# RWKV in units of 256 tokens on one chain, and the 24 matmuls of a weight panel's group kept together, in a two-layer decoder on one Trainium2 core

## The chip, the cores and the metric

The kernel runs on one core of a Trainium2 chip. A core has five engines with queues of their own: TensorE (matmuls, PE in the rows, with its weight loads shown apart as PEld), VectorE (DVE), ScalarE (ACT), GpSimd (POOL) and SyncE (SP, which issues the DMA transfers here). Each takes its instructions in the order that was fixed when the program was built, and waits on semaphores of the others. The metric is the device time of one execution in microseconds; before the change it is 3608.89 us, the median of three runs (3601.26 to 3626.65).

## The reference, cut to what matters

Two decoder layers run over 2048 prompt tokens and over 8 sample sequences of 8 tokens, with the same weights. Each layer projects its normalized input once, runs four recurrent mixers side by side (retention, HGRN2, GLA, RWKV-7), gates and joins their outputs, projects them back, and attends to 256 memory tokens.

```python
def mixer(h, l, pos, st, v_first, P):
    proj = h @ P['w_in'][l]
    p_ret, p_hgrn, p_gla, p_rwkv = jnp.split(proj, [...], axis=-1)
    ...
    o, s_hgrn = chunked_gated_linear(...)
    ...
    o_rwkv, s_rwkv, new_shift, v_first = rwkv_branch(p_rwkv, ...)
    out = jnp.concatenate([o_ret, o_hgrn, o_gla, o_rwkv], axis=-1) @ P['w_out'][l]

def rwkv7_scan(r, w, k, v, kk, a, s0):
    def step(S, inp):
        rt, wt, kt, vt, kkt, at = inp
        sa = jnp.einsum('bhvk,bhk->bhv', S, kkt)
        S = (S * wt[:, :, None, :] - sa[..., None] * (kkt * at)[:, :, None, :]
             + vt[..., None] * kt[:, :, None, :])
        return S, jnp.einsum('bhvk,bhk->bhv', S, rt)
    ...
```

## The kernel before, in words

The prompt is cut into four blocks of 512 tokens, and each layer goes through the four blocks in turn, so there are eight block steps. A block step (`block`, `gates`, `finish`) has this work:

- **Panel matmuls.** The input projection, the gates and the output projection multiply by weight panels. Each fp32 weight is split into two parts (tile `whl`, high and low) and so is the activation (`act`), and three of the four products are kept. One output group is 8 pieces of the contraction times 3 products, so 24 matmuls in a row into one PSUM tile `psd` (`group`, called by `dense_c` with 512 columns and by `dense_t` with 256). PSUM has two such tiles.
- **RWKV** (`R_rwkv`, with `invert` for the inverse of a triangular matrix by doubling). It works on units of 128 tokens: a unit holds two chunks of 64 and four heads, so the tile `NA` has four blocks on each half of the partitions. Inside `invert` the steps alternate between TensorE (`Xb,XB` and `Wb,XB` products, transpositions of `X`) and copies on VectorE and ScalarE (`Xb`, `Wb`, `XB`, a masked copy into `X`). The state `H` goes from chunk to chunk. The four units of a block are written one after the other, but odd and even units have tiles of their own (class `Turn` adds 0 or 1 to each tag) and PSUM tiles of their own (lane `a` for even units, `c` for odd ones), so two units can be under way at once.
- **GLA, HGRN, retention.** Each works on halves of 256 tokens. GLA and HGRN use `dyadic`: per level, two sets of small products (`dn_hq,dn_hf` for HGRN, 16 matmuls of 64x64 by 32 columns) go into PSUM lane `b`, masked copies put them into `sT`, and a key step and a query step on VectorE scale the operands for the next level. Then come outputs, state updates (`S_hgrn`, `S_ret`) and a head norm (`osb`, `hst`, `hss`, `rsq`, `hri`).
- **Output projection** (`w_out`), cross-attention to the memory, and the norm of the next block's input (`pre_norm`, interleaved through `ahead`).

What sets the order on an engine is a scheduler that runs when the program is built. It takes, of the instructions whose operands are there by its own clock, the one that stands first by priority; priority is the place in the code plus the offsets of the table `PRI`. `held` changes this for matmuls and transpositions: it counts matmuls that are recorded one after the other, and lifts each of them by `HOLD` except every `run[0]`-th one. A lifted matmul comes before everything else, so a run of `run[0]` matmuls can't be broken by others, and at the run's end another instruction may come in between. `run[0]` is `DENSE`, 12, for all matmuls, and `group` begins a new count.

Of the kernel before, what the change touches and what calls it, by code (L numbers as in the profile page):

```python
# [10 lines left out]
F32 = mybir.dt.float32  # L11
# [32 lines left out]
DENSE = 12  # L44
# [12 lines left out]
def shape_constants(seq, past):  # L57
    f = np.float32
    c = {}
# [67 lines left out]
    c["reset"] = np.broadcast_to((np.arange(128) % 64 != 0).astype(f), (128, 128)).copy()  # L127
    c["resets"] = np.broadcast_to((np.arange(SN) % SL != 0).astype(f), (128, SN)).copy()
    return c


class Turn:


    def __init__(self, pool, i):
        self.pool, self.i = pool, i

    def tile(self, shape, dtype, name, tag, bufs=None):
        return self.pool.tile(shape, dtype, name=name, tag=f"{tag}{self.i}", **({"bufs": bufs} if bufs else {}))
# [3 lines left out]
def decoder(ctx, tc, I, C, O):  # L143
# [73 lines left out]

    run = [DENSE, 0, None]

# [685 lines left out]
    def invert(NA, smp, wp):  # L905
# [4 lines left out]
        nb = P // 32  # L910
        blk = [slice(32 * b, 32 * b + 32) for b in range(4)]
        pair = wp.tile([128, 2, 4, 32], F32, name="X", tag="wt1")[:P]
        X, XT = pair[:, 0], pair[:, 1]
        pair = wp.tile([128, 4, 64], F32, name="XB", tag="kk")
        ND = pair[:P, 0:2].rearrange("p a (b n) -> p (a b) n", b=2)
        XB = pair.rearrange("p a n -> p (a n)")[:, 128:128 + P].rearrange("p (b n) -> p b n", b=nb)
        out = wp.tile([128, 4, 64], F32, name="XT", tag="wt2")
        flat = lambda x: x.rearrange("p q n -> p (q n)")

# [4 lines left out]
        tt(V, XT, ND, bc(K["x1"][:P].unsqueeze(1), [P, 4, 32]), ALU.mult)  # L924
        tt(V, XT, XT, bc(K["I32"][:P].unsqueeze(1), [P, 4, 32]), ALU.add)
        V.transpose(flat(X), flat(XT))
        Xb = wp.tile([128, 4, nb, 32], F32, name="Xb", tag="EA")[:P]
        Wb = wp.tile([128, nb, 4, 32], F32, name="Wb", tag="WU")
# [3 lines left out]
        def diagonal(dst, x, n):  # L932

            for b in range(n):
                o, i = dst[blk[b], :, b, :], x[blk[b]]
                if b % 2:
                    V.tensor_copy(o, i)  # L937
                else:
                    A.activation(o, i, AF.Copy)  # L939

        def turned():
            pt = PS("r")[:, :P]
            tr(pt, flat(X), P)
            diagonal(Xb, X, nb)
            A.activation(flat(XB), pt, AF.Copy)
        for li in range(1, 3 if smp else 5):
            turned()
            pw = PS("r")[:, :P].rearrange("p (b n) -> p b n", b=nb)
            for q in range(4):
                mm(flat(pw)[blk[q]], ND[:, q, :], flat(Xb[:, q]))  # L950
            diagonal(Wb, pw, 4)
            pz = PS("r")[:P, :128].rearrange("p (q n) -> p q n", q=4)
            for b in range(nb):
                mm(flat(pz)[blk[b]], XB[:, b, :], flat(Wb[:, b]))
            V.copy_predicated(X, bc(lmask[:P, li].unsqueeze(1), [P, 4, 32]), pz)  # L955
# [6 lines left out]
        low = wp.tile([128, 2, 64], F32, name="XL", tag="rx")  # L962
        G.tensor_copy(low[:, :, 32:64], bc(K["I32"].unsqueeze(1), [128, 2, 32]))
        pw = PS("r")[:, :64].rearrange("p (e n) -> p e n", e=2)
        for q in range(4):
            mm(pw[blk[q]], NA[:, q, 0, 32:64], Xb[:, q, 0:4:2, :])
        for q in range(4):
            V.tensor_copy(Wb[blk[q], 1:4:2, q, :], XB[blk[q], 1:4:2, :])
        A.activation(low[:, :, 0:32], pw, AF.Copy)
        pz = PS("r")[:, :128].rearrange("p (q n) -> p q n", q=4)  # L970
        for e in range(2):
# [1050 lines left out]
```

## Time and profile before

| what | value |
|---|---|
| median of three runs | 3608.89 us |
| the profiled execution, its own time | 3606.38 us |
| its span | 3604.6 us |
| TensorE busy | 3396.8 us (94%) |
| VectorE busy | 2280.4 us (63%) |
| ScalarE busy | 1392.1 us (39%) |
| GpSimd busy | 561.4 us (16%) |
| mean granted TensorE clock | 0.976 of full speed |
| HBM traffic | 146 GB/s over the span |

Busy time is the union of an engine's instructions. Matmuls are pipelined, and the time from the start of one to its end is longer than the distance between two starts, so a busy TensorE can hold more or fewer matmuls. The granted clock has two levels, 2.4 GHz (1.0) and 1.2 GHz (0.5). In the rows, `L230 MATMUL psd<-act,whl 128*128 128x512` is a matmul at line 230 that writes tile `psd` from `act` and `whl`, uses 128 rows by 128 columns of the array, and has 512 columns of moving data. A small fp32 matmul shows as two in the trace (`x8` for four in the code).

### The profile page before, as it was taken

The page shows a single profiled execution, that of the slowest core. Times are in us where ns is not written, and L with a number is a line of the kernel's source. Part 1 is how long each engine was busy: PE and PEld are TensorE (multiplying, and loading weights), DVE is VectorE, ACT ScalarE, POOL GpSimd, SP SyncE. Part 2 cuts the span into 40 slices and gives each one's busy share as a digit, 9 for nine tenths or more (in the row PEclk, how much of TensorE's full clock was granted, in tenths as well). Part 3 has the DMA queues.
Part 4 walks back from the last instruction along what each step waited for, and adds up shares of the span by engine and source line. Part 5 has one row for each costly group of instructions (what it writes and reads, how often), then busy time and mean ns, then how long its engine had stood idle before and what let it go on. Part 6 is the DMA issues. An engine that isn't in the chain of part 4 may idle for free.

```text
span 3604.6 us, 88705 instructions
## 1 busy us (share of the span) xinstructions
PE 3396.8 (94%) x36362; PEld 2817.2 (78%) x36362; DVE 2280.4 (63%) x7543; ACT 1392.1 (39%) x3489; POOL 561.4 (16%) x760
## 2 busy tenths in 40 slices
PE   7999999999999999999999999999889999999998
PEld 5767787777877888788877778778777778877887
DVE  4677645876337754786457865468744677547754
ACT  4452334522244324532445433453214442354323
POOL 3323331020000100110122233101200011000100
PEclk9998999999999999999999999999989999999999
DMA  6432675236652254324542348531554522542254
GB/s 190 151 107 81 187 242 193 72 100 202 212 200 72 100 192 148 113 87 171 180 159 83 103 137 267 172 132 66 160 189 167 170 86 94 193 172 86 73 199 184
DMA packets 244156, 530.92 MB, mean 147 GB/s; under 512 B 66983, under 2 KB 181927, under 8 KB 199719
## 3 DMA queue, kind: packets, MB, share of 16 engines
q1 hardware_dynamic: 243750, 525.25, 42.8%
q8 instruction: 287, 4.70, 0.5%
q14 instruction: 119, 0.97, 0.1%
HBM read 410.04 MB, written 115.16 MB: 146 GB/s over the span
## 4 chain that ended last, share of the span: by engine, by line
PE 73%; DVE 14%; ACT 5%; issue 4%; DMA 2%; POOL 1%; SPq 0%; ACTq 0%; POOLq 0%; DVEq 0%
PE psd L230 40%; PE psc L230 12%; PE psa L230 10%; PE psb L230 5%; PE psc L272 2%; PE psa L272 2%; PE psb L272 2%; DVE rsq L236 1%; DVE Wb L937 1%; DMA wraw<-in_w_in 1%; ACT Xb L939 1%; DVE hri L292 1%; DVE sT L745 1%; DVE hss L561 1%; DVE osb L236 0%
## 5 line engine op out<-in xcount | busy, mean ns | idle before, releaser
L230 PE MATMUL psd<-act,whl 128*128 128x512 f32 (+1 forms) x4032 | 1020.3, 405 | 22.7 <-DVE th L1266 9.6
L230 PEld LDWEIGHTS psd<-act,whl 128*128 128x128 f32 (+1 forms) x4032 | 751.6, 191 | 199.4 <-issue 17.4
L230 PE MATMUL psd<-whl,act 128*128 128x256 f32 x3840 | 544.7, 293 | 5.2 <-POOL whl L236 3.4
L230 PEld LDWEIGHTS psd<-whl,act 128*128 128x128 f32 x3840 | 485.9, 194 | 27.4 <-issue 9.8
L236 POOL TENSOR_TENSOR whl<-wraw,whl 128x1024 fp32r<-128x1024 f32 (+1 forms) x90 | 218.2, 2429 | 335.3 <-ACT whl L358 303.6
L230 PE MATMUL psd<-whl,oh 128*128 128x256 f32 x1152 | 211.6, 284 | 1.2 <-DMA whl<-w_w_out 1.2
L280 POOL TENSOR_TENSOR ri<-ri,mhalf 128x1 f32<-128x1 f32 (+1 forms) x87 | 49.2, 566 | 1039.4 <-DVE ri L279 1005.5
L230 PEld LDWEIGHTS psd<-whl,oh 128*128 128x128 f32 x1152 | 177.5, 189 | 2.6 <-DMA whl<-w_w_out 0.9
L230 PE MATMUL psd<-whl,ol 128*128 128x256 f32 x576 | 162.8, 283 | 0.0
L939 ACT ACTIVATE Xb<-X 32x128 f32<-32x128 f32 x324 | 99.1, 306 | 126.0 <-DVE X L955 78.1
L358 ACT ACTIVATE whl<-wraw 128x1024 fp32r<-128x1024 f32 (+1 forms) x90 | 94.1, 1049 | 124.4 <-PE psa L230 42.4
L745 DVE COPY_PREDICATED sT<-upack,psb 128x128 f32<-128x128 uint8 x320 | 92.6, 326 | 33.1 <-PE psb L230 29.5
L236 DVE TENSOR_TENSOR x<-x,psd 128x256 f32<-128x256 f32 x72 | 30.3, 421 | 128.3 <-PE psd L230 128.3
L230 PEld LDWEIGHTS psd<-whl,ol 128*128 128x128 f32 x576 | 108.6, 189 | 0.4 <-DVE ol L236 0.4
L230 PE MATMUL psb<-dn_hq,dn_hf 64*64 64x32 f32 (+1 forms) x3840 | 99.9, 225 | 7.8 <-DVE dn_hq L236 5.0
L230 PEld LDWEIGHTS psb<-dn_hq,dn_hf 64*64 64x64 f32 x3840 | 82.4, 137 | 31.0 <-issue 17.9
L435 ACT ACTIVATE xs<-xn 128x1024 f32<-128x1024 f32 (+1 forms) x34 | 35.8, 1054 | 155.4 <-PE psb L272 151.2
L1266 DVE SCALAR_TENSOR_TENSOR th<-th,psd 128x512 f32<-128x512 f32 x48 | 32.4, 686 | 91.8 <-ACT th L1265 91.8
L230 PE MATMUL psd<-hts,wraw 128*64 128x64 f32 x1984 | 84.1, 229 | 3.4 <-DVE th L1266 3.4
L230 PEld LDWEIGHTS psd<-hts,wraw 128*64 128x64 f32 x1984 | 69.9, 139 | 21.4 <-issue 11.0
L230 PE MATMUL psa<-whl,oh 128*128 128x256 f32 x448 | 82.8, 283 | 0.0
L230 PE MATMUL psc<-whl,oh 128*128 128x256 f32 x448 | 82.7, 283 | 0.0
(760 smaller groups left out, 7302.3 us busy)
## 6 DMA issues: line engine op xcount, KB each, us to landing
whl<-w_w_out SPq DMA_DIRECT2D x56, 1024.0 KB
wraw<-in_w_in SPq DMA_DIRECT2D x76, 512.0 KB
wraw<-in_w_out SPq DMA_DIRECT2D x32, 512.0 KB
w_w_out<-whl SPq DMA_DIRECT2D x16, 1024.0 KB
x<-x SPq DMA_DIRECT2D x32, 512.0 KB
whl<-w_rw_r SPq DMA_DIRECT2D x12, 1024.0 KB
whl<-w_rw_k SPq DMA_DIRECT2D x12, 1024.0 KB
whl<-w_rw_v SPq DMA_DIRECT2D x12, 1024.0 KB
```

The source lines that it names most:

```text
L230: PE.matmul(out, lhsT=lhsT, rhs=rhs, start=start, stop=stop, skip_group_check=True)
L236: e.tensor_tensor(out, a, b, op)
L272: PE.transpose(out, in_, ident[:rows, :rows])
L280: G.tensor_tensor(y, y, mhalf[:P], ALU.pow)
L292: V.scalar_tensor_tensor(y, t, 1.5, y, ALU.add, ALU.mult)
L358: A.activation(hl[:, 0], raw, AF.Copy)
L435: A.activation(out, xt, AF.Square, accum_out=ss[:P])
L561: V.tensor_reduce(ss[:P, :n4], sq[:P, :n4], AX.X, ALU.add)
L745: V.copy_predicated(out, bc(mk, [P, w, 32 // s, s]), ps)
L937: V.tensor_copy(o, i)
L939: A.activation(o, i, AF.Copy)
L1266: V.scalar_tensor_tensor(th, th, 1.0, x, ALU.add, ALU.mult)
```

## The change

RWKV's unit becomes 256 tokens (`nu = 2`, so four chunks and, in `invert`, eight blocks `m` in two groups `ng`), so a block has two units, and they share one set of tiles and both lanes: one unit runs after the other. Operations on VectorE and ScalarE are twice as wide and half as many; products that have their own 32 or 64 columns stay as many. `DENSE` becomes 24, and it holds only inside `group` and for each token tile in `w_out`; all other matmuls get runs of `SMALL`, 48. The core of the diff:

```diff
-DENSE = 12
+DENSE = 24
+SMALL = 48
...
-class Turn:
...
-    run = [DENSE, 0, None]
+    run = [SMALL, 0, None]
...
     def group(out, pairs):
         n = len(pairs)
-        run[2] = None
+        run[:] = DENSE, 0, None
         for i, (a, b) in enumerate(pairs):
             mm(out, a, b, i == 0, i == n - 1)
-        run[2] = None
+        run[:] = SMALL, 0, None
...
+        m = NA.shape[1]
+        ng = m // 4
...
         def turned():
-            pt = PS("r")[:, :P]
-            tr(pt, flat(X), P)
-            diagonal(Xb, X, nb)
-            A.activation(flat(XB), pt, AF.Copy)
+            pt = PS("r")[:, :ng * P]
+            for g in range(ng):
+                tr(pt[:, g * P:(g + 1) * P], flat(four(X, g)), P)
+            diagonal(lambda b: Xb[blk[b], :, b, :], lambda b: X[blk[b]], nb)
+            A.activation(XB.rearrange("p g b n -> p (g b n)"), pt, AF.Copy)
         for li in range(1, 3 if smp else 5):
             turned()
-            pw = PS("r")[:, :P].rearrange("p (b n) -> p b n", b=nb)
-            for q in range(4):
-                mm(flat(pw)[blk[q]], ND[:, q, :], flat(Xb[:, q]))
-            diagonal(Wb, pw, 4)
...
+            pw = PS("r")[:, :ng * P].rearrange("p (g b n) -> p g b n", g=ng, b=nb)
+            for g in range(ng):
+                for q in range(4):
+                    mm(flat(pw[:, g])[blk[q]], ND[:, 4 * g + q, :], flat(Xb[:, 4 * g + q]))
+            diagonal(lambda q: Wb[blk[q], :, :, q, :], lambda q: pw[blk[q]], 4)
...
-        nu = 1
-        P = n = 64 * ne
+        nu = 1 if smp else 2
+        P = 64 * ne
+        n = nu * P
...
-            for u in range(NT):
-                wp = Turn(wk, u % 2)
+            for u in range(NT // 2):
                 vfb = None
                 if l > 0:
-                    vfb = wp.tile([128, 2, 128], F32, name="vfb", tag="vT")
-                    dma(vfb, vf[b][:, :, u * 128:(u + 1) * 128])
-                with on_lane("ac"[u % 2]):
-                    R_rwkv(l, pr, st["H"], rk, on["rwkv"], wp, u, vfb)
+                    vfb = wk.tile([128, 2, 256], F32, name="vfb", tag="vT")
+                    dma(vfb, vf[b][:, :, u * 256:(u + 1) * 256])
+                R_rwkv(l, pr, st["H"], rk, on["rwkv"], wk, u, vfb)
...
                     for t in ts:
+                        run[:] = DENSE, 0, None
                         for n, k in enumerate(ks):
```

The order of TensorE in the third token block of layer 0, inside RWKV's `invert`, where its levels stand between GLA products (`qx`, `dn_qk`) and panels (`whl`). First before:

```order
L230 MATMUL psc<-Wb,XB 32x128 x4
L230 MATMUL psb<-qx_15036,dn_qk 64x64 x8
L230 MATMUL psa<-Wb,XL 64x128 x2
L230 MATMUL psa<-vT,LK 64x64 x8
L272 MATMUL psa<-fpack,ar 128x128 x2
L272 MATMUL psc<-fpack,X 128x128
L230 MATMUL psc<-Xb,XB 32x128 x4
L230 MATMUL psd<-whl,act 128x256 x12
L230 MATMUL psa<-Z,XT 64x128 x8
L230 MATMUL psc<-Wb,XB 32x128 x4
```

The same engine and block after the change:

```order
L221 MATMUL psa<-Xb,XB 32x128 x8
L221 MATMUL psd<-whl,act 128x256 x24
L221 MATMUL psc<-Wb,XB 32x128 x8
L221 MATMUL psb<-qx_13483,dn_qk 64x64 x8
L221 MATMUL psd<-whl,act 128x256 x24
L263 MATMUL psa<-fpack,X 128x128 x2
L221 MATMUL psc<-Xb,XB 32x128 x8
```

Where two units in lanes `a` and `c` stood between each other with half a panel group, there is now one unit with twice the matmuls in a step, and a whole group behind nearly every step.

The second place, on TensorE in the same block, is the second half of HGRN (`dn_hq,dn_hf`, the products of its levels) with retention (`S_ret`, `dn_rv`, `rqT`). First before:

```order
L230 MATMUL psb<-dn_hq,dn_hf 64x32 x16
L230 MATMUL psd<-act,whl 128x512 x12
L230 MATMUL psb<-dn_hq,dn_hf 64x32 x16
L230 MATMUL psd<-act,whl 128x512 x12
L230 MATMUL psb<-dn_hq,dn_hf 64x32 x16
L230 MATMUL psd<-act,whl 128x512 x12
L230 MATMUL psb<-dn_hq,dn_hf 64x32 x16
L230 MATMUL psd<-act,whl 128x512 x12
L230 MATMUL psb<-dn_hq,dn_hf 64x64 x8
```

The same engine and place after the change:

```order
L221 MATMUL psb<-dn_hq,dn_hf 64x32 x16
L221 MATMUL psc<-S_ret,rqT 64x128 x2
L221 MATMUL psc<-dn_rv,sT 64x64 x4
L221 MATMUL psb<-dn_hq,dn_hf 64x32 x16
L221 MATMUL psc<-S_ret,rqT 64x128 x2
L221 MATMUL psc<-dn_rv,sT 64x64 x4
L263 MATMUL psc<-fpack,dn_rq 128x128 x4
L221 MATMUL psb<-dn_hq,dn_hf 64x32 x80
L263 MATMUL psa<-fpack,osb 128x128 x4
L263 MATMUL psa<-fpack,dn_rk 128x128 x4
L221 MATMUL psb<-dn_hq,dn_hf 64x64 x8
```

The panel groups that stood between the levels now stand earlier, between steps of RWKV and GLA, and the levels follow each other with only small matmuls between them (`x80` is five levels in a row).

## Rows read from the trace of the kernel before

**Rows 1.** The page: the span, and each engine's busy time, share and instructions.
```profile
span 3604.6 us, 88705 instructions
PE 3396.8 (94%) x36362; PEld 2817.2 (78%) x36362; DVE 2280.4 (63%) x7543; ACT 1392.1 (39%) x3489; POOL 561.4 (16%) x760
```

**Rows 2.** Busy time by stretch: third block; VectorE's busiest 120 us; 2603 to 2639.
```profile
core 0: us, PE busy (x) PEld busy (x) DVE busy (x) ACT busy (x) POOL busy (x), PEclk, DMA share, GB/s
954.00:1321.00 367.00, 358.21 (x3875) 287.83 (x3875) 229.82 (x821) 147.57 (x381) 30.58 (x68) 1.00 0.40 138
...
600.00:720.00 120.00, 116.33 (x1404) 89.72 (x1403) 96.47 (x393) 63.27 (x188) 12.84 (x35) 1.00 0.31 108
...
2603.00:2639.00 36.00, 19.38 (x217) 16.79 (x215) 24.09 (x69) 9.39 (x16) 2.70 (x4) 0.69 0.24 81
```

**Rows 3.** TensorE's waits: who waited for whom; total us, times, longest.
```profile
PE psb L272 <- DVE xs L439: 19.7, 5, 5.9
...
PE psc L272 <- DVE osb L236: 10.2, 5, 6.8
...
PE psb L230 <- DVE dn_hq L236: 5.0, 8, 1.6
```

**Rows 4.** Timeline, 2400 to 2420: start, us, engine, line, operation [idle before <-releaser].
```profile
2401.20 0.43 PE L230 MATMUL psa<-Wb,XB 128*32 128x128 f32 x8
2401.44 0.40 PE L230 MATMUL psc<-Xb,XB 128*32 128x128 f32 x8
2401.77 0.44 PE L272 MATMUL psb<-fpack,dn_qk 128*128 128x128 f32 x2
2402.04 0.33 PE L272 MATMUL psa<-fpack,X 128*128 128x128 f32 x1
2402.30 0.44 PE L230 MATMUL psb<-S_gla,qx 128*64 128x128 f32 x4
2402.57 0.40 PE L230 MATMUL psb<-dn_gv,sT 128*64 128x64 f32 x8
2402.80 0.39 PE L230 MATMUL psb<-S_gla,qx 128*64 128x128 f32 x4
2403.03 0.40 PE L230 MATMUL psb<-dn_gv,sT 128*64 128x64 f32 x8
2403.36 0.32 PE L230 MATMUL psa<-Xb,NA 128*32 128x64 f32 x8
2403.61 3.01 PE L230 MATMUL psd<-act,whl 128*128 128x512 f32 x12
2406.55 0.20 PEld L230 LDWEIGHTS psa<-Wb,XL 128*64 128x64 f32 x4 [0.35 <-issue]
2406.55 0.44 PE L230 MATMUL psa<-Wb,XL 128*64 128x128 f32 x4
```

**Rows 5.** Timeline of TensorE, 2639 to 2660: whole groups of 24 panel matmuls.
```profile
2639.05 6.36 PE L230 MATMUL psd<-act,whl 128*128 128x512 f32 x24
2646.82 5.73 PE L230 MATMUL psd<-act,whl 128*128 128x512 f32 x24 [0.33 <-DVE th L1266]
```

**Rows 6.** Timeline, 2606 to 2642: the head norm at the end of retention.
```profile
2633.32 0.69 DVE L236 TENSOR_TENSOR osb<-osb,hri 128x512 f32<-128x512 f32 x1
2634.16 1.09 PE L272 MATMUL psc<-fpack,osb 128*128 128x128 f32 x4 [6.83 <-DVE osb L236]
```

**Rows 7.** Instructions by line, whole span: count, busy us, mean ns, idle before.
```profile
L230 PE MATMUL psd<-act,whl 128*128 128x512 f32 (+1 forms) x4032 | 1020.3, 405 | 22.7 <-DVE th L1266 9.6 <-DVE carry L539 9.1 <-DVE act L236 1.5
L230 PE MATMUL psb<-dn_hq,dn_hf 64*64 64x32 f32 (+1 forms) x3840 | 99.9, 225 | 7.8 <-DVE dn_hq L236 5.0 <-DVE carry L539 1.3 <-DVE dn_hf L830 0.9
L745 DVE COPY_PREDICATED sT<-upack,psb 128x128 f32<-128x128 uint8 x320 | 92.6, 326 | 33.1 <-PE psb L230 29.5
L236 DVE TENSOR_TENSOR dn_hf<-dn_hf,tot 128x256 f32<-128x256 f32 x96 | 46.7, 487 | 6.8 <-PE psb L230 4.6 <-issue 2.1
L236 DVE TENSOR_TENSOR osb<-osb,hri 128x512 f32<-128x512 f32 (+1 forms) x54 | 36.8, 681 | 1.5
```

More of the change, by code (lines that the diff above doesn't have):

```diff
@@ L126, in shape_constants @@
     c["half"] = ((part // 32 % 2)[:, None] == np.arange(2)[None, :]).astype(f)
-    c["reset"] = np.broadcast_to((np.arange(128) % 64 != 0).astype(f), (128, 128)).copy()
+    c["reset"] = np.broadcast_to((np.arange(256) % 64 != 0).astype(f), (128, 256)).copy()
     c["resets"] = np.broadcast_to((np.arange(SN) % SL != 0).astype(f), (128, SN)).copy()
     return c
-class Turn:
[L135 to L139, printed above, removed]
 @with_exitstack
@@ L1141, in R_rwkv @@
-            ps = PS("r").rearrange("p (q n) -> p q n", q=4)
+            ps = PS("t").rearrange("p (u i g d) -> p u i g d", u=nu, i=2, g=2)
+            for u in range(nu):
+                for i in range(2):
+                    tr(ps[:, u, i].rearrange("p g d -> p (g d)"), al[:, i, u * 128:(u + 1) * 128], 128)
+            A.activation(Z[:, :, 0, :].rearrange("p (g q) d -> p g q d", g=2), ps.rearrange("p u i g d -> p g (u i) d"), AF.Copy)
+            ps = [PS("r").rearrange("p (q n) -> p q n", q=nq) for _ in range(2)]
@@ L1164, in R_rwkv @@
-            for e in range(2):
-                tt(V, DB[:, :, e], pg[e], bc(eb[:, :, e, 64:65], [128, 2, 64]), ALU.mult)
-            Hn = wp.tile([128, 2, 2, 64], F32, name="Hn", tag="wt2")
+            GT = wp.tile([128, 2, ng, 64], F32, name="GT", tag="kk")
+            DB = wp.tile([128, 2, ng, 64], F32, name="DB", tag="rx")
+            pr = [PS("r").rearrange("p (i u j n) -> p i u j n", i=2, u=nu, j=2) for _ in range(2)]
+            ipe = [(i, u, p, e, p * nq + u * 2 + i, slice(64 * p, 64 * p + 64), slice(64 * e, 64 * e + 64))
+                   for u in range(nu) for i in range(2) for e in range(2) for p in range(2)]
@@ new lines, in R_rwkv @@
+            pg = [PS("r")[:, :nu * 128].rearrange("p (i u n) -> p i u n", i=2, u=nu) for _ in range(2)]
+            for i, u, p, e, q, hp, ep in ipe:
+                mm(pg[e][hp, i, u, :], kT[ep, u, hs(i, p)], vT[ep, u, hs(i, p)], True, False)
+                mm(pg[e][hp, i, u, :], bT[ep, q, :], U[ep, q, 1, :], False, True)
+            for e in range(2):
+                tt(V, by(DB)[:, :, :, e], pg[e], bc(by(eb)[:, :, :, e, 64:65], [128, 2, nu, 64]), ALU.mult)
+            Hn = wp.tile([128, ng, 2, 64], F32, name="Hn", tag="wt2")
@@ L1167, in R_rwkv @@
             V.tensor_copy(Hn[:, 0], Hst)
-            H = [Hn[:, 0], Hn[:, 1], Hst]
-            for j in range(2):
+            H = [Hn[:, j] for j in range(ng)] + [Hst]
+            for j in range(ng):
                 ph = PS("r")[:, :128].rearrange("p (i n) -> p i n", i=2)
```

98 lines of the change are left out of this document (45 added, 53 removed).

## The prediction

> **What bounds the kernel now.** I read the page's busy shares first, then one block's stretch, then the waits, then the order of the instructions. TensorE is busy 3396.8 us of a span of 3604.6 [rows 1], so it is idle for only 208 us. In the third token block of layer 0, which has no sample rows and no first loads, TensorE is busy 358.2 of 367.0 us and VectorE 229.8 [rows 2]. VectorE's busiest 120 us hold 96.5 us of work, 80%, with TensorE at 97% beside it. So TensorE sets the pace, and VectorE's long chains (HGRN, retention, RWKV) are hidden because a run of panel matmuls stands between nearly every two of their steps. The waits agree: none on a VectorE line exceeds 20 us [rows 3].
>
> There is one place where no panel matmul is left, 2603 to 2639 us. There TensorE is busy 19.4 of 36 us, VectorE 24.1 (67%), and the granted clock is 0.69 [rows 2]. TensorE waits 6.83 us at a time for a retention head norm [rows 6]. This is what a chain costs without cover, and the forecast rests on it.
>
> **The change, part by part.**
>
> *Wider RWKV steps.* The built orders hold 1496 fewer VectorE and 760 fewer ScalarE instructions, because two units of 128 tokens become one of 256. TensorE's matmuls stay (36362 now, 36138 by the order). On the path I cost this at nothing: TensorE at 358 of 367 us is the cover [rows 2], and the saved operations run beside it. Where that cover is gone, the narrower load counts, and it is counted there below.
>
> *Fewer breaks between panel matmuls and small ones.* Over the whole orders, the array's tile shape (128x128, 64x64, 128x32 and so on) changes from one matmul to the next 2049 times before and 1450 times now: 599 fewer. For the price: 24 panel matmuls in a row take 5.73 us [rows 5]; without the last one's 0.41 us [rows 7] that is 0.232 us from start to start. Twelve are then worth 2.78 us, but the small matmul behind the run that starts at 2403.61 comes 2.94 us after its start [rows 4], so leaving a run costs 0.16 us more. Another change of shape, from the transposition at 2402.04 to the next group, takes 0.26 us, where a small matmul in a group takes about 0.05. I take 0.16: 599 x 0.16 = 96 us gained. The bounds are 0.10 and 0.22, so 60 to 130 us.
>
> What the trace shows at such a change: the weight loads stand idle for 0.35 us behind the run of twelve, with no releaser but issue [rows 4]. The Trainium skill (TensorEngine Tiling, Key Properties) says that changing the tiling mode, not just the tile, drains the engine. By that rule alone the change only saves drains. By the rows, the drains are one term of several, and the larger one has the other sign.
>
> *Where the panel matmuls went.* Each time TensorE takes a panel group it now takes all 24, so for each small step twice as much of it is used up. The second fence of the order shows the consequence: in the second half of HGRN, runs of twelve panel matmuls stood between the levels, and now there is nothing between them. Counted over both orders, the longest stretches without a panel matmul held 384, 322 and 303 matmuls before. Now there are eight, one for each block of each layer, with 694, 788, 1112, 711, 697, 902, 1112 and 979: 6995 matmuls. They hold the end of the RWKV chain, most of HGRN (2016 of its 3840 product matmuls) and all or most of retention. The panels of the gates and of the output projection stand behind each stretch in TensorE's order, so a late head norm delays them too.
>
> *What such a stretch takes.* On TensorE alone little: from 2401.20 to 2403.61 us 51 small matmuls start [rows 4], 0.047 us each, so 6995 take 330 us. That is what they cost before, inside the cover. On VectorE, 1580 instructions lie between the first and the last wait of these stretches. A mean instruction is 229.8/821 = 0.28 us in the whole block and 24.1/69 = 0.35 us in the uncovered stretch [rows 2], since tail instructions are wide (0.49 us for an HGRN step, 0.68 us for a head norm's pass, against 0.33 us for a masked copy [rows 7]). I take 0.29 (many are the tiny ones of the norms), 460 us of work; the bounds are 442 and 551. VectorE can't be busy all the time there: an HGRN level is two masked copies, a key step and a query step, each level's products wait for both steps, and the next copies wait for the products. The rows give two shares: 80% with three chains under way and 67% with one [rows 2]. Here two or three chains run for most of the stretch and one at its end; I take 80%: 460/0.80 = 575 us. So the tails cost 575 - 330 = 245 us more. The bounds: 442 us at 95% is 465, so 135 more; 460 at 67% is 687, so 357 more.
>
> *Smaller terms.* The 36 us stretch of before is swallowed by one of the eight: its idle 16.6 us go (36.0 less 19.4 [rows 2]). After an idle stretch the clock has to come back: the first run of 24 took 6.36 us against 5.73 [rows 5], so eight times 0.63, 5 us. In the covered part, one chain instead of two, with a full run between steps: a step may come later, or TensorE may wait for a double-wide operation. A run of 24 with 512 columns is 5.73 us, longer than any step of a few operations of 0.3 to 0.5 us [rows 7], but the 256-column runs are about half, and the norm of the keys is a dozen operations. I take 10 us, between nothing and 40. Weight transfers keep their number and size and get the same panels a little faster; they kept up with TensorE at 98% in the block above, and I take nothing.
>
> **Sum.** The profiled execution took 3606.4 us (span 3604.6 and 1.8 around it); the median is 2.5 higher. 3606.4 - 96 + 245 - 17 + 5 + 10 = 3753, and with the median's 2.5: 3756 us, 4.1% slower.
>
> **Rivals.**
>
> 1. *Only the breaks count (faster).* If VectorE reaches these tails with most of its work done, or the fewer and wider RWKV operations let the chains end while panels last, TensorE stays covered: 3606 - 96 = 3510 us, with no tails. This is what the rule of the Trainium skill (TensorEngine Tiling, Key Properties) would make of the change. For it: the block of rows 2 has VectorE at 63%, so there is slack. Against it: the order is fixed when the program is built, TensorE takes its instructions in that order, and products of HGRN can't start before VectorE has made their operands. It becomes true when the eight stretches take under about 95 us more than 330 in all, that is when VectorE would do its 460 us of work in 425, which it can't. Only if the instructions that I put in the stretches were far cheaper than the rows say could it win. Chance 0.07.
>
> 2. *The tails are short (within 1%).* With VectorE at 95% and 442 us of work, tails cost 135 more, and with 130 saved at the breaks: 3606 - 130 + 135 - 17 = 3594 to, with 96 saved, 3628 us. For it: three chains side by side leave few gaps. Against it: no stretch of 120 us in the trace has VectorE above 80%, and retention alone got 67%. Chance 0.13.
>
> 3. *The tails are long (slower still).* If they run like the stretch from 2603 to 2639 throughout, at 67%, and the small matmuls at half clock lengthen each round trip: 3606 - 96 + 357 - 17 + 5 + 40 = 3895 us. For it: the clock of 0.69 there, and that in a queue that runs in order one late head norm holds up the other chain's step behind it. Against it: that stretch had a single chain. Chance 0.2.
>
> **How the numbers follow.** The forecast, tails at about 80%, has 0.6; the rivals 0.07, 0.13 and 0.2. The predicted time is that of the forecast, 3756 us. Its own range, from 0.9 to 0.72 of VectorE in the tails with 460 us of work (511 to 639 us), is 3690 to 3820. Leaving out the faster rival and the far half of the third gives 3620 to 3870. About 1% is what a measurement of this kernel can tell from no change. Faster by over 1% is rival 1 alone, 0.07, slower than 3645 us takes the forecast and rival 3, together 0.8; within 1% is rival 2, 0.13.
>
> **What would show it.** Tails: in each block a stretch of some 55 to 90 us before the output projection with TensorE busy about half, VectorE near 80% and a granted clock well under 1; among the waits, TensorE for `dn_hq`, `dn_hf` and `osb`, tens of us each where 5 to 10 stood before. Breaks: runs of 24 panel matmuls of 5.7 us, and outside the tails each block shorter than before. The widths: VectorE's busy time lower by some 200 us in all. The prediction is wrong if TensorE's idle time stays near 208 us, or if VectorE shows over 90% in the tails; and if TensorE waits long for RWKV tiles in the covered part, the term of 10 us was the wrong one.

## The result, and the profile after

The changed kernel takes 3904.73 us (median of 6 runs, 3898.89 to 3908.82) against 3607.92 us before: a ratio of 1.0819, 95% interval 1.0803 to 1.0835. It is slower by 297 us where 148 were forecast, and above the range's upper end of 3870 us.

The page of the changed kernel: the span, each engine's busy time, and two rows of the 40 slices (tenths of TensorE's busy share and of its granted clock).

```profile
span 3903.3 us, 85580 instructions
...
PE 3491.6 (89%) x36138; PEld 2947.8 (76%) x36138; DVE 2122.5 (54%) x6047; ACT 1276.6 (33%) x2729; POOL 552.9 (14%) x680
...
PE   7998699986999979997999978999789998899978
...
PEclk9999599986999979997999977999679998899979
```

TensorE is idle for 411.7 us of the span, twice the 207.8 of [rows 1]. The idle time stands in dips, about one for each block, and the clock dips with it. VectorE's total fell by 158 us; it is not short of time on average.

The eight longest stretches without a panel matmul (tails), found by the order and timed from the last panel matmul ahead to the first one behind, and below them the covered stretch ahead of the third tail. Three more stretches hold 320 to 496 matmuls, but take only 13 to 19 us each and are not counted. Columns: window, length, busy us and count by engine, granted clock, DMA share, GB/s.

```profile
core 0: us, PE busy (x) PEld busy (x) DVE busy (x) ACT busy (x) POOL busy (x), PEclk, DMA share, GB/s
379.40:485.00 105.60, 71.79 (x697) 51.67 (x696) 55.10 (x180) 25.68 (x54) 18.73 (x23) 0.59 0.19 53
846.70:963.90 117.20, 74.65 (x791) 56.65 (x789) 70.31 (x221) 20.77 (x43) 21.08 (x29) 0.57 0.22 55
1333.70:1426.40 92.70, 66.83 (x1114) 55.61 (x1112) 65.18 (x212) 26.67 (x56) 8.59 (x16) 0.69 0.10 32
1771.10:1842.50 71.40, 46.86 (x713) 38.82 (x711) 51.59 (x168) 16.65 (x34) 8.37 (x19) 0.69 0.07 20
2269.30:2386.30 117.00, 73.11 (x700) 51.97 (x698) 64.42 (x195) 28.96 (x64) 24.87 (x26) 0.62 0.21 60
2753.50:2872.90 119.40, 74.76 (x905) 56.55 (x903) 73.02 (x243) 22.23 (x45) 19.68 (x29) 0.60 0.19 53
3256.70:3351.30 94.60, 66.78 (x1115) 55.89 (x1113) 63.92 (x212) 26.64 (x56) 8.36 (x16) 0.68 0.09 32
3693.30:3771.20 77.90, 53.80 (x981) 45.03 (x979) 54.77 (x187) 19.89 (x40) 7.30 (x14) 0.76 0.07 21
sum 795.80, PE 528.58 PEld 412.18 DVE 498.31 ACT 187.49 POOL 116.98; mean PE 66.07 PEld 51.52 DVE 62.29 ACT 23.44 POOL 14.62
...
963.90:1333.70 369.80, 364.73 (x3376) 309.35 (x3374) 168.66 (x488) 116.00 (x258) 23.76 (x45) 0.99 0.49 170
```

The tails take 796 us, with VectorE busy for 498 of them, 62.6%, less than the 67% of the stretch from 2603 to 2639 in [rows 2]. TensorE is busy for 66% of the tails, and for 98.6% of the covered stretch, at a clock of 0.99. The runs of 24 are as fast as in [rows 5], 5.73 us.

TensorE's waits (who for whom; total us, times, longest), the answer to [rows 3]. First the head norms before, in all three lanes, then the changed kernel:

```profile
PE psc L272 <- DVE osb L236: 10.2, 5, 6.8
...
PE psb L272 <- DVE osb L236: 8.6, 6, 3.7
...
PE psa L272 <- DVE osb L236: 5.3, 4, 2.5
```

```profile
PE psa L263 <- DVE osb L227: 40.5, 11, 6.8
PE psc L263 <- DVE osb L227: 34.4, 8, 6.8
PE psb L263 <- DVE osb L227: 26.6, 10, 6.3
...
PE psb L221 <- DVE dn_hq L227: 20.3, 18, 2.7
```

The head norms (`osb`) now hold TensorE for 101.5 us in 29 waits, against 24.1 us in 15 before. The longest wait is the 6.8 us of [rows 6], as before; what changed is how often a long one is met.

How such a tail ends, from the timeline of the changed kernel (start, us, engine, line, operation [idle before <-releaser]); TensorE's weight loads, DMA and a few operations of the next block's norm are left out:

```profile
1413.46 0.60 ACT L627 ACTIVATE osb<-psc 128x512 f32<-128x512 f32 x1 [4.10 <-PE psc L221]
...
1415.40 0.68 DVE L546 TENSOR_REDUCE hst<-osb 128x8 f32<-128x512 f32 x1
...
1416.24 0.42 DVE L227 TENSOR_TENSOR xg<-psb,cols 128x256 f32<-128x256 f32 x1 [0.15 <-PE psb L263]
...
1416.98 0.68 DVE L227 TENSOR_TENSOR osb<-osb,hst 128x512 f32<-128x512 f32 x1
1417.58 0.42 DVE L227 TENSOR_TENSOR xg<-psb,cols 128x256 f32<-128x256 f32 x1
1418.04 0.63 ACT L550 ACTIVATE hsq<-osb 128x512 f32<-128x512 f32 x1 [3.98 <-DVE xg L227]
1418.70 0.69 DVE L552 TENSOR_REDUCE hss<-hsq 128x8 f32<-128x512 f32 x1 [0.70 <-ACT hsq L550]
...
1419.42 0.17 DVE L275 TENSOR_SCALAR rsq<-hss 128x8 f32<-128x8 f32 x1
...
1422.39 0.17 DVE L283 SCALAR_TENSOR_TENSOR hri<-rsq,hri 128x8 f32<-128x8 f32 x1
1422.59 0.69 DVE L227 TENSOR_TENSOR osb<-osb,hri 128x512 f32<-128x512 f32 x1
...
1423.43 1.09 PE L263 MATMUL psa<-fpack,osb 128*128 128x128 f32 x4
```

Retention's last output leaves PSUM at 1413.46 us, and its transposition starts at 1423.43: ten microseconds of one short operation after another. The reciprocal square root alone lasts from 1419.42 to 1422.56, eleven operations of 0.17 us in line, with others between them. In the meantime TensorE has only twelve transpositions for the next block's norm to do.

Beside it, the tail's small matmuls are slower. First three groups in the third tail, then the same in the kernel with 256-token units and runs of 12 (e3 below), where panels stand around nearly all of them (line, operation, count, busy us, mean ns):

```profile
L221 PE MATMUL psc<-S_ret,rqT 128*64 128x128 f32 x32 | 4.9, 404 | 0.0
...
L221 PE MATMUL psc<-dn_rv,sT 128*64 128x64 f32 x64 | 4.7, 294 | 0.0
...
L221 PE MATMUL psc<-rqT,rkT 64*128 64x128 f32 x16 | 4.1, 438 | 0.0
```

```profile
L221 PE MATMUL psc<-S_ret,rqT 128*64 128x128 f32 x192 | 20.5, 293 | 0.0
...
L221 PE MATMUL psc<-rqT,rkT 64*128 64x128 f32 x128 | 20.3, 303 | 2.4 <-DVE rqT L227 1.6 <-ACT rkT L856 0.7
...
L221 PE MATMUL psc<-dn_rv,sT 128*64 128x64 f32 x384 | 20.2, 228 | 0.1
```

The matmuls are 29 to 45% longer. A mean granted clock between 0.5 and 1 is a mix of the two levels, 1.2 and 2.4 GHz, and the trace shows that this is the reason: in the tails a matmul of 128x64 by 128 columns takes 273 ns (median) where the clock is 1.0 and 421 where it is 0.5, one of 64x64 by 32 columns 219 and 291, and 273 and 219 are also what they take outside the tails.

### The profile page after: what moved, and what is told of

Same layout as the page of the kernel before. It is cut to its first block, busy times and chain, and to the rows that moved or that the text cites. A ratio compares the mean times of both kernels' runs of the same rounds, so it can differ in the third digit from the quotient of the medians.

```text
span 3903.3 us, 85580 instructions
## 1 busy us (share of the span) xinstructions
PE 3491.6 (89%) x36138; PEld 2947.8 (76%) x36138; DVE 2122.5 (54%) x6047; ACT 1276.6 (33%) x2729; POOL 552.9 (14%) x680
## 5 line engine op out<-in xcount | busy, mean ns | idle before, releaser
L221 PE MATMUL psd<-act,whl 128*128 128x512 f32 (+1 forms) x4032 | 986.7, 401 | 25.4 <-DVE th L1266 12.8
L221 PE MATMUL psd<-whl,act 128*128 128x256 f32 x3840 | 515.1, 290 | 14.8 <-POOL whl L227 6.7
L221 PE MATMUL psb<-dn_hq,dn_hf 64*64 64x32 f32 (+1 forms) x3840 | 108.0, 250 | 41.8 <-DVE dn_hq L227 19.8
L221 PEld LDWEIGHTS psb<-dn_hq,dn_hf 64*64 64x64 f32 x3840 | 92.8, 165 | 68.7 <-issue 51.2
L932 ACT ACTIVATE Xb<-X 32x256 f32<-32x256 f32 (+1 forms) x164 | 67.4, 411 | 119.0 <-DVE X L951 69.4
L739 POOL MEMSET sT<- 64x512 f32 x32 | 16.6, 520 | 540.7 <-ACT sT L738 473.8
```

The costliest lines, as they stand in the source:

```text
L221: PE.matmul(out, lhsT=lhsT, rhs=rhs, start=start, stop=stop, skip_group_check=True)
L739: G.memset(sT[64:128, :, 0, :], 0.0)
L932: A.activation(dst(b), src(b), AF.Copy)
```

## The experiments

All ratios are to the kernel before, measured on the same chip. Two numbers in the table are worked out. **Floor**: every pair of successive matmuls, sorted by kind, is given the lower quartile of its start-to-start spacing in the trace of before, and these are summed over the kernel's own order. It is an estimate of what TensorE needs when nothing keeps it waiting. **Excess**: the trace's start-to-start time less that floor, for windows of 200 matmuls, apart by whether fewer than 20 of them are panel matmuls ("bare") or not. The level of both depends on how finely the matmuls are sorted: by array shape and columns alone, the floor is 2728 us for before and 2631 for the change, 97 apart as against 96 in the table, and the bare excess rises by 427 us from one to the other as against 354. So only differences between kernels are read from them. A bare stretch that is shorter than a window, or the end of a longer one, can count under "else".

| run | RWKV | group / small runs | us | ratio, 95% | floor | excess bare | excess else |
|---|---|---|---|---|---|---|---|
| before | 128 | 12 / 12 | 3608 | 1 | 3375 | 28 | 179 |
| e3 | 256 | 12 / 12 | 3575.93 | 0.9907 (0.9882-0.9933) | 3298 | 28 | 224 |
| e7 | 256 | 8 / 12 | 3575.52 | 0.9901 (0.9869-0.9933) | 3293 | 29 | 239 |
| e4 | 256 | 6 / 48 | 3581.95 | 0.9933 (0.9907-0.9958) | 3300 | 55 | 219 |
| e1 | 256 | 12 / 48 | 3618.29 | 1.0019 (1.0005-1.0033) | 3292 | 43 | 252 |
| e6 | 256 | 16 / 12 | 3638.73 | 1.0078 (1.0052-1.0105) | 3292 | 62 | 274 |
| e5 | 256 | 24 / 12 | 3828.95 | 1.0597 (1.0568-1.0626) | 3281 | 315 | 211 |
| the change | 256 | 24 / 48 | 3904.73 | 1.0819 (1.0803-1.0835) | 3279 | 382 | 224 |
| e12 | 128 | 24 / 12 | 3886.93 | 1.0763 (1.0740-1.0786) | 3363 | 249 | 249 |
| e2 | 128 | 24 / 48 | 3900.51 | 1.0798 (1.0769-1.0827) | 3365 | 241 | 270 |
| e13 | 256 | 24, gates 4 / 12 | 3727.08 | 1.0318 (1.0285-1.0350) | 3291 | 176 | 235 |
| e14 | 256 | 12, gates 4 / 12 | 3570.06 | 0.9880 (0.9854-0.9905) | 3299 | 29 | 221 |
| e16 | 256 | 8, gates 4 / 12 | 3561.98 | 0.9888 (0.9857-0.9919) | 3293 | 28 | 220 |

**Theory A**: the unbroken groups use the panels up while the chains are still under way, and what is left of the chains then runs alone, step after step. **Rival B**: the single RWKV chain of 256 leaves the tails, whatever the runs.

### e1, e2 and e3: the two halves of the change apart

```diff
 e1 and e3
-DENSE = 24
+DENSE = 12
 e3 alone
-SMALL = 48
+SMALL = 12
```

```diff
 e2, on the kernel before
-DENSE = 12
+DENSE = 24
+SMALL = 48
...
-    run = [DENSE, 0, None]
+    run = [SMALL, 0, None]
...
-        run[2] = None
+        run[:] = DENSE, 0, None
...
+                        run[:] = DENSE, 0, None
```

> The change without its long runs: RWKV in one chain of 256 tokens, but a panel's group is broken after 12 matmuls as before. Its order has no panel-free stretch of 600 trace matmuls (the longest 314; the change has eight of 694 to 1112), and 1655 changes of array tile shape (2049 before, 1488 in the change). Theory A (the unbroken groups use the panels up and leave tails): about 3510 us (3440 to 3570), from the 3375 us that all TensorE matmuls took at their unstalled spacing in the trace of before, less 83 us for the fewer and wider matmuls and tile changes, plus 150 to 230 us of stalls that both traces have outside tails. Rival B (the single chain of 256 leaves the tails, whatever the runs): 3750 us or more, with TensorE's waits for the head norms (osb) still near 100 us.

> The kernel before with the runs alone: 128-token RWKV units in two alternating lanes stay, the 24 matmuls of a panel's group are not broken, small matmuls run up to 48. Its order has eight panel-free stretches of 413 to 964 trace matmuls and three of 303 to 379, 5602 in all (the kernel before: three of 303 to 384). Theory A: 3850 us (3750 to 3930): the tails of the change cost 796 us against 323 at TensorE's unstalled spacing, 0.068 us a matmul more, here some 340 to 380 us. Rival B (the single chain makes the tails long; two lanes fill each other's waits): tails near TensorE's own pace, 3600 to 3680 us.

> RWKV in one chain of 256 alone, all runs of 12 as before (groups and small matmuls). Order: longest panel-free stretch 344, 1652 changes of tile shape. Theory A: like the run with groups of 12 and small runs of 48, 3510 us (3440 to 3570), within 0.5% of it: the runs of small matmuls matter little. Rival B: 3750 us or more. Rival C (longer runs of small matmuls are what brings the change its gain outside the tails): 30 us or more slower than the run with 48.

The wide RWKV alone is 33 us faster than before (e3), the runs alone are 291 us slower (e2). B falls, and so does the idea that two lanes would fill each other's waits. With two lanes of 128, e2 has tails too; the sum over its eight longest:

```profile
sum 551.00, PE 353.78 PEld 280.95 DVE 355.24 ACT 127.54 POOL 61.37; mean PE 44.22 PEld 35.12 DVE 44.41 ACT 15.94 POOL 7.67
```

VectorE's share is 64% in them, as in the change. They are shorter, 551 us against 796, so the single chain does lengthen the tails once the runs are unbroken: on top of e3 the runs cost 329 us, on the kernel before 291. For e2, theory A's 3750 to 3930 held, though its centre was 50 us low. Of e3's expectation the direction held; it missed the size (3576 where 3440 to 3570 stood): the floor falls by 77 us, but the excess rises by 45 (224 against 179). It is not RWKV's steps that TensorE waits for there: its waits for `osb` rise from 24 to 54 us, and a second bare stretch has come, 36.9 us long from 2145 us on, with a wait of 8.3 us for `osb` in it.

e1 was expected at 3510 and came out at 3618: the small runs of 48, thought harmless, cost 42 us over e3. Much of it stands in stretches without a panel again. The longest of e1, with 314 matmuls, and below it the one at the same place in e3, with 220:

```profile
2589.50:2647.90 58.40, 35.35 (x316) 27.66 (x314) 32.94 (x98) 11.05 (x20) 6.22 (x8) 0.64 0.23 70
...
2582.30:2620.70 38.40, 19.37 (x223) 16.73 (x221) 25.17 (x70) 8.39 (x15) 4.18 (x6) 0.71 0.24 80
```

The first takes 20 us more than the second. The next three of e1 take 45.4, 32.4 and 30.1 us, and the next three of e3 36.9, 20.6 and 16.0.

### e4 to e7 and e12: the length of the runs

The edits are the two numbers of the table, on the change (e4 to e7) and on e2's kernel (e12: `SMALL = 12`).

> RWKV in one chain of 256, a panel's group broken after 6 matmuls, small runs of 48. The order has no panel-free stretch of 300 trace matmuls, 1728 changes of tile shape (1655 with 12) and 748 pieces of panel work (649 with 12). Theory A: finer pieces spread the panels better; with breaks at 0.16 us the 73 more cost 12 us, cover gained perhaps 10 to 40 us: 3500 us (3430 to 3570), within 1% of the run with 12. If breaks were dear (as the change assumes): 30 us or more slower than the run with 12. Rival B: 3750 us or more.

> The change with its small matmuls in runs of 12 instead of 48; a panel's group of 24 stays unbroken. The order keeps the tails: eleven panel-free stretches of 380 to 1130 trace matmuls, 8187 in all (the change: eleven, 8139). Theory A (unbroken groups make the tails): within 1% of the change, 3870 to 3920 us. Rival D (the runs of 48 small matmuls, which cost 42 us in the comparison with groups of 12, are half of the loss here too): 3800 us or less.

> RWKV in one chain of 256, small runs of 12, a panel's group broken once, after 16 of 24. Theory A, by the order: no stretch over 312 trace matmuls, 9007 matmuls in stretches over 100 (8326 with 12, 13741 with 24), so the loss has a threshold: 3590 us (3560 to 3640). Rival E (each waiting step of a chain pays for the length of the run ahead of it, covered or not, so that the loss grows evenly with the run's length): a third of the way from 3576 to 3905, 3685 us.

> RWKV in one chain of 256, small runs of 12, a panel's group broken after 8 and 16. The order has no panel-free stretch of 300 (one of 344 with 12), 7144 matmuls in stretches over 100 (8326 with 12), 1644 changes of tile shape (1652), 714 pieces of panel work (645). Theory A: 10 to 30 us less stall than with 12, 69 more pieces at 0.25 us cost 17 us: 3565 us (3540 to 3590). If breaks are dear: 3600 us or more.

> The kernel before (RWKV of 128 in two lanes) with the unbroken groups of 24 alone; small matmuls stay in runs of 12. Order: thirteen panel-free stretches of 303 to 1061, 6934 trace matmuls in all (with small runs of 48: eleven, 5602), 1889 changes of tile shape (1960). With one chain of 256 the small runs of 48 cost 76 us on top of the unbroken groups. If they make the tails slow in the same way here: 3820 to 3860 us (3900 with 48). If the stretches' lengths in the order decide alone, at 0.05 us a panel-free matmul: 3900 to 3970 us.

With small runs of 12, group runs of 8, 12, 16 and 24 give 3575.5, 3575.9, 3638.7 and 3829.0 us. The loss is not even in the run's length (rival E had 3685 for 16, and a third of the way from e3 to e5 itself would be 3660), since nothing is lost from 8 to 12. Nor is it a clean threshold: 3639 is at the upper end of theory A's 3560 to 3640, 49 us above its centre. Up to 12 the cover lasts, then it fails faster and faster. e7 against e3 shows a cheap break: 69 more pieces of panel work, no change in the time. e4's expectation of 3500 (3430 to 3570) fell (3582), as did rival D: e5 is not under 3800.

But e5 is 76 us below the change, more than the 1% that theory A allowed. The small runs matter in the tails. The sum over e5's eight tails:

```profile
sum 736.50, PE 493.41 PEld 387.64 DVE 469.64 ACT 176.23 POOL 103.29; mean PE 61.68 PEld 48.46 DVE 58.70 ACT 22.03 POOL 12.91
```

They hold 6923 matmuls (6995 in the change) and take 736 us (796). Fewer matmuls account for some 8 of the 59 us; for the rest the likely reason is that TensorE takes its instructions in order, so that a chain whose operands are ready stands behind up to 48 small matmuls of another. That is argued, not shown. In the narrow kernel the small runs cost only 14 us (e12 against e2), so neither of the two accounts given for e12 hit: 3887 lies between them.

### e8, e9, e10, e11, e15: the norm in the chain

e8 (on the change) and e15 (on e3) shorten the reciprocal square root; e9 (on the change), e10 (on e3) and e11 (on e7) replace it.

```diff
 e8, e15
-        for _ in range(3):
+        for _ in range(1):
```

```diff
 e9, e10, e11
-        if n == 1:
-            V.tensor_scalar(y, in_, mul, add, ALU.mult, ALU.add)
-            G.tensor_tensor(y, y, mhalf[:P], ALU.pow)
-            return
+        V.tensor_scalar(y, in_, mul, add, ALU.mult, ALU.add)
+        tt(G, y, y, mhalf[:P] if n == 1 else bc(mhalf[:P], [P, n]), ALU.pow)
+        return
```

> The change with one Newton step instead of three in the reciprocal square root of the head norms and of cross attention's norm (the output is then only approximate): six tiny VectorE instructions of 0.16 to 0.2 us less per norm, 43 norms in the eight tails, 43 us. The order's tails shrink a little too (panel-free stretches over 300: 7258 trace matmuls, 8139 in the change). If the tails go at the pace of one step after another through VectorE (theory A): 35 to 45 us for the norms and up to 60 us for the shorter stretches, 3820 us (3790 to 3865). If TensorE at its lower clock sets the tails' pace (rival F): the shorter stretches alone, and the time per panel-free matmul stays, 3850 to 3900 us.

> RWKV in one chain of 256, all runs of 12, with one Newton step instead of three in the reciprocal square roots (the output is only approximate). In the change the same edit gave 104 us. If it gave them because there the norm's VectorE steps stand alone on the path (theory A): where panels cover, 0 to 30 us, 3560 us (3545 to 3577). If the norms are on the path everywhere (rival I): 80 us or more, below 3500 us.

With six operations of 0.17 us less per norm the change is 104 us faster (3800.39, ratio 1.0517, 1.0483 to 1.0551), and the kernel with covered chains only 23 (3553.17 against 3575.93). That fits steps which are on the path where no panel stands beside them and mostly hidden where one does. But the shorter chain also changed the built order, and only a part of the 104 us is the steps themselves. The sum over the eight tails of e8:

```profile
sum 654.30, PE 449.23 PEld 352.46 DVE 400.34 ACT 160.87 POOL 95.01; mean PE 56.15 PEld 44.06 DVE 50.04 ACT 20.11 POOL 11.88
```

The order's tails shrank too, to 6042 matmuls, 0.864 of the change's. At the change's time per matmul (rival F) they would take 687 us; theory A's 40 us for the norms makes that 647; they take 654. So some 33 us speak for the steps, and over 100 for the shorter stretches; of the 142 us that the tails lost, some 40 came back outside them. VectorE's share is 0.61 to 0.64 in the tails of the change, e5 and e8 alike (498/796, 470/736, 400/654): the tails are about 1.6 times as long as VectorE's work in them. TensorE's share is as even (529/796, 493/736, 449/654: 0.66 to 0.69), so this does not tell which of the two sets the pace; it shows that neither is busy throughout.

> The change with the head norms' reciprocal square root as one VectorE and one GpSimd instruction (a power of -0.5, exact) instead of 11 VectorE ones: ten instructions of 0.16 to 0.2 us less in a row per norm, some 1.7 us, against one GpSimd instruction of about 0.6 us and a hop. If the tails go step after step through VectorE (theory A): more than the version with one Newton step gave (3800), 3775 us (3740 to 3800), though GpSimd's weight splits of 2.43 us each may stand ahead of the power. If VectorE's count of instructions in the tails were not what mattered there, but the accuracy-free shorter order: like the version with one Newton step, 3800 to 3830. If the splits on GpSimd's queue delay it: 3850 or more.

> RWKV in one chain of 256, all runs of 12, and the head norms' root as a power on GpSimd. Here the panels cover the chains: the 278 us between 3576 and TensorE's unstalled 3298 are short waits. Theory A: a shorter chain lowers these by a tenth or so, 3550 us (3520 to 3575), against 3576 with the 11 VectorE instructions. Rival G (in covered stretches a norm's length costs nothing): 3570 to 3585 us. Rival H (the power waits behind GpSimd's 2.43 us weight splits): 3590 us or more.

> As the run with all runs of 12 and the power on GpSimd, but a panel's group is broken after 8 and 16. Order: 1713 changes of tile shape (1646 with 12), 730 pieces of panel work (646), three panel-free stretches of 300 to 392 (one of 344). Theory A: within 0.5% of the run with 12, 3550 us (3520 to 3585), as 8 and 12 were alike without the power (3575.5 and 3575.9). If the price of a break counts: 20 us or more slower than with 12.

The power on GpSimd misses everything that was hoped of it: 3862.38 us on the change (1.0695, 1.0669 to 1.0720), 3627.32 on e3 (1.0033, 1.0003 to 1.0063), 3667.88 on e7 (1.0158, 1.0136 to 1.0181). The costliest lines of e10 show why (count, busy us, mean ns, idle before and its releaser):

```profile
L227 POOL TENSOR_TENSOR hri<-hri,mhalf 128x8 f32<-128x8 f32 (+1 forms) x72 | 114.3, 1588 | 536.4 <-DVE hri L269 513.0 <-DVE ri L269 14.8 <-DMA wraw<-in_w_in 4.9
...
L227 DVE TENSOR_TENSOR osb<-osb,hri 128x512 f32<-128x512 f32 (+1 forms) x54 | 53.0, 982 | 95.0 <-POOL hri L227 95.0
```

The power takes 1.59 us in the mean (1.64 with 8 columns, the median) and not the 0.6 that was assumed from one column, and VectorE waits 95.0 us for it. The ten operations that it replaces take 1.7 us, so its length alone gains nothing, and does not explain e10's loss of 51 us either. Rival H came out in size, but the power seldom stands behind a weight split: that holds for 2 of the 72 powers in e10's trace, and the median power starts 0.08 us behind the VectorE operation that it waits for. It is the pass behind the power that meets the split. From e10's timeline:

```profile
450.76 1.63 POOL L227 TENSOR_TENSOR hri<-hri,mhalf 128x8 f32<-128x8 f32 x1 [2.55 <-DVE hri L269]
...
452.36 2.34 POOL L227 TENSOR_TENSOR whl<-wraw,whl 128x1024 fp32r<-128x1024 f32 x1
452.43 2.82 DVE L227 TENSOR_TENSOR osb<-osb,hri 128x512 f32<-128x512 f32 x1 [1.81 <-POOL hri L227]
```

GpSimd goes on to its next operation when the power is done, and the norm's last pass, 0.69 us by itself, takes 2.82 us beside it. Of the 64 such passes of 512 columns in e10, 15 are stretched like this, 6 of them to 2.82 us, 18 us in all; in e3 it is one, by 0.3 us. Where the rest of the 51 us comes from is not shown. e11 is a miss too: it was expected within 0.5% of e10 and is 41 us slower, as if breaks were dear, where without the power 8 and 12 were alike. That stays open, and the price of a break with it.

### e13, e14, e16, e17: panels kept for the end

The eight gate panels at the end of each block are broken into runs of 4 and so spread over the chains' last steps.

```diff
 e13 (e14: DENSE = 12, e16: DENSE = 8)
+GATES = 4
...
-        run[:] = DENSE, 0, None
+        run[:] = part[0], 0, None
...
+                part[0] = GATES
                 proj_c(cn, i * 128, ev, evs, smp, hts)
+                part[0] = DENSE
```

> RWKV in one chain of 256, small runs of 12, groups of 24 unbroken except in the eight gate panels at the end of each block, which are broken into runs of 4. The order's panel-free stretches over 300 fall from eleven (8187 trace matmuls) to eight (3211), the longest from 1130 to 506; changes of tile shape rise from 1429 to 1560. Theory A (what costs is work left without a panel beside it): at 0.052 us a panel-free matmul (tails of the run with 24 and 12: 790 us, 362 of them TensorE's own, over 8187) 259 us less than 3829 us, 3570 us (3560 to 3680 as the remaining stretches and the 100 to 300 long ones count). Rival E (every chain step pays for the unbroken 24 ahead of it): 23 of 31 panels still cost it, 3760 us or more.

> RWKV in one chain of 256, all runs of 12, the eight gate panels of each block in runs of 4. Order: one stretch over 300 (344, as with 12), 7752 matmuls in stretches over 100 (8326), 1675 changes of tile shape (1652). Theory A: the little left to cover gives 10 to 25 us, 3560 us (3545 to 3580). If the finer pieces cost more than their cover: 3585 us or more.

> RWKV in one chain of 256, small runs of 12, a panel's group broken after 8 and 16, the gate panels in runs of 4. The order has the fewest panel-free matmuls of all: no stretch of 300, 6924 in stretches over 100 (7752 with 12 and 4, 8326 with 12 alone), at 1656 changes of tile shape. Theory A: at 0.03 to 0.05 us for each of the 800 fewer, 3535 us (3520 to 3565) against 3570. If cover is saturated there (8 and 12 were alike before): 3565 to 3580 us.

> RWKV in one chain of 256, all runs of 12, gate panels in runs of 4, and two Newton steps instead of three in the reciprocal square roots (a relative error of some millionths). With one step the norms gave 23 us where panels cover the chains; half of it here, 3558 us (3545 to 3572). If the changed order (one stretch of 422 instead of 344, 8230 matmuls in stretches over 100 instead of 7752) outweighs it: 3575 us or more.

Breaking a quarter of the panels gives back 102 of the 253 us that separate e5 from e3. Neither account had 3727. The excess says how to read it: 139 us less in bare windows, 24 more elsewhere, 10 more floor. So the loss does sit in bare stretches and not in every unbroken group (rival E), but the estimate by stretches over 300 was too bright, since pieces of 200 to 300 matmuls remain that take far more than their floor (194 us against 97 by the table's sorting).

e14 and e16 are the fastest with the computation in full: 3570.06 and 3561.98 us, 1.2 and 1.1% faster than before. The two can't be told apart, and their intervals overlap those of e3 and e7, so what the finer gate panels add to runs of 12 or 8 is not clear of the noise. e17 is e14 with two Newton steps: 3549.11 us, ratio 0.9838 (0.9818 to 0.9857), as expected. The bare excess is at 25 to 29 us in all of these. That speaks for saturated cover, in which finer runs have nothing more to give, though e16's time, between its two expectations, does not decide it.

## Why the forecast missed

**The direction and the mechanism held.** Tails in each block before the output projection, a low clock, waits for `osb` and `dn_hq`: all are there. e2, e3 and e12 show that the runs of 24 make them.

**The failed step is the tails' size.** The forecast divided 460 us of VectorE's work by a share of 0.80, 575 us. Measured: 498 us at 0.626, 796 us. Of the 221 us too few, the share makes 160 (460/0.626 = 735) and the work 61 (38 us more, at the same share: 1618 instructions of 0.31 us where 1580 of 0.29 were counted). The 0.80 came from a stretch of [rows 2] in which panels filled TensorE's queue. There TensorE always had something to do until a chain's next operands were ready. With the panels gone it has not, and near the end of a tail one norm remains, ten microseconds long. The nearest row was the one bare stretch of before, 67%, and it was set aside because only one chain ran in it. Two or three chains did no better: 0.63 here and 0.64 in e2. The range failed with it: its bounds were 551 us for the work and 67% for the share, but never both at once; together they are 822 us of tails, and the measured 796 lie inside. Rival 3 read the share at 67%, came to 3895 us, 10 us from the result, and had a chance of 0.2. That closeness is luck: its tails are 687 us, 109 too short, and outside them it gained 68 us where 168 were gained.

**The lower clock** is in that share: 29 to 45% longer matmuls in each round trip. How much of the 796 us it makes stays open; it was not tried apart from the rest. An estimate from the trace bounds it: TensorE is busy at the lower level for 399 us of the tails, which would be 90 to 124 us less at the higher one, if all of it lay on the path. Even so the tails would be 672 us or more, where 575 were forecast.

**The term for breaks had the right size, but little of it comes from the runs.** 96 us were to come from 599 fewer changes of tile shape (561 in the count that the expectations use, 2049 to 1488). The floor did fall by 96 (3375 to 3279), but 77 of them come with the 256-token units while the groups stay in runs of 12 (e3): 397 fewer changes, 0.19 us each if the changes are all of it, which is not shown apart from the fewer matmuls. The runs of 24 and 48 add 19, at 164 fewer changes (1652 to 1488), about 0.12 us each. Rival 1, and with it the rule in the Trainium skill (TensorEngine Tiling (Array Packing), Key Properties) that a change of tiling mode drains the engine, points the right way, but what it saves here is a fifteenth of what the missing cover costs (e5 against e3: 17 us of floor for 253 us). The forecast took the wider steps to be free and counted their fewer changes under breaks; alone they make the kernel 33 us faster (e3).

**Outside the tails** 98 us were to be gained (96 + 17 - 5 - 10), and 168 were: 3886 - 796 = 3090 us from the first matmul to the last, against 3588 - 330 = 3258 before. The floor accounts for 89 of it. The rest, 79, is nearly the fall of the excess there, 133 us against 207 before the change in all: waits that used to be scattered among the panels now seem to stand in the tails. Only the 17 us of one stretch had been counted for that. So the forecast was 221 us too low in the tails and 70 too high outside them, and the 149 us that it missed are about the difference of the two. By these numbers the whole is 3606 + (796 - 330) - 168 = 3904; that it closes proves nothing, since the 168 is taken from the same two traces.

**The smaller points.** Runs of 24 at 5.73 us: right. VectorE lower by some 200 us: 158, for 1496 fewer instructions 0.106 us each. The 10 us for longer RWKV steps: e3 has 45 us more excess beside the panels, above the bound of 40, but its longer waits are for `osb`, not for RWKV's tiles. The tails last 71 to 119 us where 55 to 90 stood, with TensorE busy for 66% and not half, and `dn_hf` hardly shows among the waits (3.6 us). The 80% was also called the highest of any 120 us; from 1945.5 to 2065.5 VectorE is busy for 100.25, 84%, with TensorE at 92%. That would have made the forecast lower still.

## What to carry to other kernels

Work that hides a dependent chain is a stock: a longer run spends more of it per step of the chain, so count in the built order what the last steps will have beside them before lengthening a run. Price the uncovered part by an uncovered stretch of the trace, however short, and not by the share that an engine reaches under cover: here VectorE's share was 67% in 36 us before, and 61 to 64% over the tails of four kernels. One stretch is a rough guide all the same: single tails of the change run from 52 to 72%. Small runs at the end of the stock (here eight panels in runs of 4) cost next to nothing and keep it for the chain's last steps.

## What the rows showed of the hardware

A VectorE operation with two operands in SBUF waits for a GpSimd multiply or subtraction on SBUF that has started before it. From the timeline of the changed kernel (the first line is two operations):

```profile
1378.22 1.36 POOL L227 TENSOR_TENSOR rkd<-dn_rk,fpack 128x256 f32<-128x256 f32 x2
1378.30 0.81 DVE L227 TENSOR_TENSOR dn_hf<-dn_hf,tot 128x256 f32<-128x256 f32 x1
1379.03 0.83 DVE L227 TENSOR_TENSOR dn_hq<-dn_hq,tot 128x256 f32<-128x256 f32 x1
...
1381.81 0.42 DVE L227 TENSOR_TENSOR dn_hf<-dn_hf,tot 128x256 f32<-128x256 f32 x1
1382.14 0.42 DVE L227 TENSOR_TENSOR dn_hq<-dn_hq,tot 128x256 f32<-128x256 f32 x1
```

The same two steps take 0.81 and 0.83 us while GpSimd works and 0.42 us one level later. The longer the GpSimd operation, the longer the wait: in the same trace such a step takes up to 2.46 us beside a weight split (`whl`), and in e10 a pass that starts 0.07 us behind a split of 2.34 us ends 0.55 us after it. The Trainium skill (SBUF — State Buffer, SBUF: two separate sides) says that a VectorE operation with two SBUF inputs and a GpSimd one lock each other out; for these operations the trace agrees. For the power it does not: in e10, 20 such VectorE operations of 512 columns start while a power runs, and none is more than 0.03 us longer than usual, while all 15 that start while a weight split runs are, by 0.86 to 2.14 us. So in e10 the norm's last pass, which follows the power and meets what GpSimd does next, takes 982 ns in the mean against 681 in [rows 7].
